# Hybrid encoder on one core: modulation's sums pinned in VectorE's order, three kinds of loads moved to later jobs

## The chip, the cores and the metric

One Trainium2 chip, one of its cores. The metric is the device time of one launch in microseconds (us). The kernel before was run three times.

## What is computed

Two layers (DEPTH = 2) of a hybrid encoder over one sequence of 256 tokens with 1024 features, all in f32. Cut to what matters here:

```python
for l in range(DEPTH):
    mod = (silu(c) @ w_ada[l] + b_ada[l]).reshape(bsz, 6, 1, D_MODEL)      # modulation
    shift1, scale1, gate1 = mod[:, 0], mod[:, 1], mod[:, 2]
    shift2, scale2, gate2 = mod[:, 3], mod[:, 4], mod[:, 5]
    h = x * (1.0 + scale1) + shift1
    aq, ak, av, bq, bk, bv, cq, ck, cv, dx, dg, gl = split(h @ w_in[l])
    oa = window_gqa(rope(aq), rope(ak), av)
    ob = neighbourhood_attention(bq, bk, bv, b_rpb[l])                      # its biases
    oc = diff_attention(rope(cq), rope(ck), cv)
    od = rg_lru_branch(dx, dg, d_wa[l], d_wx[l])                            # recurrence, its weights
    mix = sum(sigmoid(gl) * (stack(oa, ob, oc, od) @ w_branch[l])) @ w_out[l]
    x = layer_norm(ALPHA * x + gate1 * mix)
    x = layer_norm(ALPHA * x + gate2 * peer_ffn(x * (1.0 + scale2) + shift2))
```

## The kernel before, in words

**Jobs.** The program is one list of jobs, built in order and run by the loop at the end of `_body`. Most jobs are one product: a 512 KB block of weights (`src`) is loaded into one of three `raw` buffers, split by ScalarE into a high part `whi` (L230) and by VectorE into the rest `wlo` (L233), and multiplied by TensorE in three passes (`prod`, L238 to L240: 24 matmuls of 256 columns). Loads run three blocks ahead and splits two jobs ahead. A load into a `raw` buffer (L1218) waits for the `wlo` split that read that buffer last. Layer 0 starts with eight `start_chunk` jobs, which make the modulated input `h`; then come 38 jobs of `w_in` for the four mixers, 32 for the gates, 16 of `w_branch` and 8 of `w_out`; this stretch is called mixing here. After it come LayerNorm, 16 query jobs, 128 jobs that read `p_u`, and 128 that read `p_v` (V jobs). Layer 1 repeats mixing and what follows.

**Modulation.** `ada_load` loads a 512 KB column block of `w_ada` (L254), `ada_sum` multiplies it on VectorE by silu(c), adds along the row and leaves one column of `mods` (L259, shown as CUSTOM_DVE_ANT_0 in the trace, as ISA in the instruction order). The eight first pairs (shift1 and scale1 of layer 0) are summed in `start_chunk`. The 24 next (gate1, shift2, scale2 of layer 0) are loaded and summed during layer 0's mixing: `stage(i)` hangs on the job `w[8 * i // 3]`, `staged(i)` on the job five later, with two buffers in `mixA`. All others (56) are loaded and summed beside V jobs into the tile `adav`, `vstage` on one job and the sum four jobs later. Layer 1's mixing holds no modulation.

**Who sets the order.** The program's text gives each instruction a place, and a scheduler then orders each engine's queue by its own estimate of when operands are ready; each engine runs its queue strictly in that order. `V` is VectorE, and its instructions can be moved. `VB` (class `InOrder`) issues the same instruction through `tc.keep_in_program_order`, so that it keeps its place in the text. In the trace all instructions issued through `VB` or `SB` carry line L93. The loads all go through one queue, SyncE's (SP), also in order: one that waits for its buffer holds all behind it.

**Mixing's own loads.** `mix_begin` loads the recurrence's weights `wblk` (1 MB, L437) into the buffer that held `x`, the cosines (256 KB, L442) and, by `load_bias`, the neighbourhood biases (two of 1 MB, L588). Rotary jobs (`rope_post`) copy rows by four small DMAs each (L460) and then do two products and a sum on VectorE (L465 to L467).

Of the kernel before, what the change touches and what calls it, by code (L numbers as in the profile page):

```python
# [18 lines left out]
OP = mybir.AluOpType  # L19
# [97 lines left out]
def _body(tc, nc, A, pp, big, hp, st, wk, ps, dr, stop, dump):  # L117
    V, S, PE = nc.vector, nc.scalar, nc.tensor
    VB, SB = InOrder(tc, V), InOrder(tc, S)
# [25 lines left out]
    state = {"left": [], "leaving": []}  # L145
# [83 lines left out]
    def split_hi(hi, src, scale=1.0):  # L229
        return S.activation(hi, src, AF.Copy, scale=scale)  # L230

    def split_lo(lo, src, hi):
        return V.tensor_tensor(lo, src, hi.bitcast(F32), op=OP.subtract)  # L233

    def prod(out, whi, wlo, x, n):

        for c in range(n):
            PE.matmul(out, wlo(c), x(c)[:, 0], start=c == 0, stop=False)  # L238
            PE.matmul(out, whi(c), x(c)[:, 1], start=False, stop=False)  # L239
            PE.matmul(out, whi(c), x(c)[:, 0], start=False, stop=c == n - 1)  # L240
# [12 lines left out]
            with behind(state["load"]):  # L253
                nc.sync.dma_start(buf[:, k], A["w_ada"][l, i, :, k * D:(k + 1) * D])  # L254

    def ada_sum(l, i, buf, ks=(0, 1)):
        for k in ks:
            n = ADA[2 * i + k]
            V.tensor_tensor_reduce(out=buf[:, k], in0=buf[:, k], in1=state["cact"], scale=1.0,  # L259
                                   scalar=prm[:, P_BADA + 48 * l + n:P_BADA + 48 * l + n + 1],  # L260
                                   op0=OP.mult, op1=OP.add, accum_out=mods[l][:, n:n + 1])

    def mains(ks):

        state["banks"] = cycle(ks)

    def main_bank(shape, name):
        return bank(next(state["banks"]), shape, name=name)
# [25 lines left out]
    def new_h():  # L294
        return hp.tile([128, NC8, 2, T], F32R, name="h", tag="h")
# [86 lines left out]
    jobs = []  # L382
# [7 lines left out]
            before[n + 1 + i].hooks.append(lambda i=i, j=j: area_split(i, j))  # L390

    def start_chunk(m):
        ada_sum(0, m, state["ada"][:, m])
        if m == 0:
            state["h"] = new_h()
        hx = state["h"]
        x = state["x"][:, m]
        V.tensor_scalar(opsc[:, m:m + 1], mods[0][:, 8 + m:9 + m], 1.0, None, op0=OP.add)
        h = wk.tile([128, T], F32, name="hf", tag="t1k", bufs=6)
        S.activation(h, x, AF.Identity, scale=opsc[:, m:m + 1], bias=mods[0][:, m:m + 1])  # L400
        split_hi(hx[:, m, 0], h)
        split_lo(hx[:, m, 1], h, hx[:, m, 0])
# [20 lines left out]
    def layer(l):  # L423
# [3 lines left out]
        def mix_begin():  # L427
            m = big.tile([128, 64, T], F32, name="mixA", tag="gA")
            state["m"] = m
            state["bh"] = [big.tile([128, 12, 2, T], F32R, name="mixB0", tag="gB0"), None]  # L430
            state["gt"] = big.tile([128, 32, T], F32, name="mixG", tag="gB1")
            mains((0, 1, 5))
            state["ab"] = []
            state["scans"] = 0
            mf = m.rearrange("p a b -> p (a b)")
            state["wblk"] = big.tile([128, 16, 128], F32, name="wblk", tag="gB2")
            nc.sync.dma_start(state["wblk"], A["d_w"][l])  # L437
            state["dxp"] = mf[:, 34 * 256:34 * 256 + 4 * 260].rearrange("p (c t) -> p c t", c=4)
            V.memset(state["dxp"][:, :, 0:2], 0.0)
            V.memset(state["dxp"][:, :, 258:259], 0.0)  # L440

            nc.sync.dma_start(state["gt"][:, 6:8].rearrange("p a b -> p (a b)"), A["cst"][:, C_COS:C_COS + 2 * T])  # L442
            load_bias()

        def w_in_job(n, post):
            def mm(hi, lo):
                out = main_bank([128, T], name="main")
                state["out"] = out
                x = state["h"]
                prod(out, lambda c: hi[:, c], lambda c: lo[:, c], lambda c: x[:, c], NC8)  # L450
                return out
            return Job(src=A["w_in"][l, n], mm=mm, post=post)

        def rope_post(n, slot, scale):
            def post(out):
                dst = state["m"][:, slot]
                rot = wk.tile([128, T], F32, name="ropet", tag="t1k", bufs=6)
                S.activation(dst, out, AF.Copy, scale=scale)
                for a, b in ((0, 32), (32, 0), (64, 96), (96, 64)):
                    nc.sync.dma_start(rot[a:a + 32], dst[b:b + 32])  # L460

                def gen(lane):
                    yield 0.0
                    cos, sin = state["gt"][:, 6], state["gt"][:, 7]
                    V.tensor_tensor(dst, dst, cos, op=OP.mult)  # L465
                    V.tensor_tensor(rot, rot, sin, op=OP.mult)
                    V.tensor_tensor(dst, dst, rot, op=OP.add)  # L467
                state["leaving"].append(gen)
            return post

        def copy_post(slot, scale=1.0):
            def post(out):
                S.activation(state["m"][:, slot], out, AF.Copy, scale=scale)
            return post

        def v_post(dst):
            def post(out):
                raw = wk.tile([128, T], F32, name="vx", tag="t1k", bufs=6)
                S.activation(raw, out, AF.Copy)

                def gen(lane):
                    yield 0.0
                    p = bank(2, [128, 2, 128], name="vt")
                    for t in range(2):
                        PE.transpose(p[:, t], raw[:, t * 128:(t + 1) * 128], ident)
                    V.tensor_copy(dst(), p)
                state["leaving"].append(gen)
            return post

        def vdst(slot, n, k):  # L490
            def f():
                v = state["m"][:, slot:slot + n].rearrange("p a b -> p (a b)").rearrange("p (t e) -> p t e", t=2)
                return v[:, :, k * 128:(k + 1) * 128]
            return f
# [89 lines left out]
        def load_bias():  # L584
            b = state["m"][:, 39:55].rearrange("p a b -> p (a b)").rearrange("p (t h k) -> p t h k", h=8, t=2)
            state["bias"] = b
            for t in range(2):
                nc.sync.dma_start(b[:, t].rearrange("p h k -> p (h k)"), A["rpb"][l, t])  # L588
# [54 lines left out]
        def lru(lane):  # L643
# [28 lines left out]
            for d, (tr, ti, aa) in enumerate(parts):  # L672
                for c in range(4):
# [12 lines left out]
                    yield 0.4, 2.8  # L686

        jobs.append(Job(func=mix_begin))
        first = len(jobs)
        def add(name, *gens):  # L690
# [7 lines left out]
            jobs.append(w_in_job(DG + c, gelu_post(30 + c)))  # L698
        for c in range(4):
            jobs.append(w_in_job(AQ + c, rope_post(AQ + c, c, 0.125)))  # L700
        jobs.append(w_in_job(AK, rope_post(AK, 4, 1.0)))
        jobs.append(w_in_job(AV, v_post(vdst(21, 1, 0))))
        for c in range(4):
# [5 lines left out]
        add("lru", lru)  # L709
        for c in range(4):  # L710
            jobs.append(w_in_job(BQ + c, copy_post(5 + c, 0.125)))
        for c in range(4):
            jobs.append(w_in_job(BK + c, copy_post(9 + c)))
        for c in range(4):
# [75 lines left out]
        def staged(i):  # L790
            buf = state["m"][:, 55:63].rearrange("p (a b) c -> p a (b c)", a=2)
            ada_sum(l, 8 + i // 2, buf, (i % 2,))
        w = [j for j in jobs[first:] if j.src is not None][4:]
        for i in range(24 if l == 0 else 0):
            w[8 * i // 3].hooks.append(lambda i=i: stage(i))
            w[8 * i // 3 + 5].hooks.append(lambda i=i: staged(i))
# [349 lines left out]
        vjobs = []  # L1146
        todo = [(l, 20 + i) for i in range(4)] + ([(l + 1, i) for i in range(20)] if l + 1 < DEPTH else [])

        def vstage(i, k):
            if i == k == 0:  # L1150
                both = hp.tile([128, 2, 2, D], F32, name="adav", tag="h")
                for n in range(2):
                    state["ada", n] = both[:, n]
            ada_load(*todo[i], state["ada", i % 2], k)
# [7 lines left out]
        for i in range(len(todo)):  # L1162
            for k in range(2):
                n = (10 if len(todo) < 12 else 5) * i + 2 * k
                vjobs[n].hooks.append(lambda i=i, k=k: vstage(i, k))
                vjobs[n + 4].hooks.append(lambda i=i, k=k: ada_sum(*todo[i], state["ada", i % 2], (k,)))

        if l + 1 < DEPTH:
            state["vjobs"] = vjobs
# [22 lines left out]
    for m in range(NC8):  # L1192
        jobs.append(Job(func=lambda m=m: start_chunk(m)))
    jobs.append(Job(func=start_end))
    jobs.append(Job(func=late_setup))
    for l in range(DEPTH):
        layer(l)
# [4 lines left out]
    if stop is not None:  # L1202
        jobs = jobs[:stop(jobs)]
# [44 lines left out]
    k = 0  # L1248
    last = None
    for i, j in enumerate(jobs):  # L1250
# [29 lines left out]
        out = j.mm(hi, lo)  # L1280
# [93 lines left out]
```

## Time and profile before

| what | us |
|---|---|
| three runs: median (lowest to highest) | 2356.8 (2355.9 to 2358.27) |
| the profiled execution: its own time | 2358.0 |
| the profiled execution: span of the core's instructions | 2356.2 |
| TensorE busy (14440 matmuls) | 2275.3 |
| VectorE busy | 1813.7 |
| ScalarE busy | 1414.0 |
| granted TensorE clock, mean over the span | 0.986 of full |

The profiled execution lies 1.2 us above the median. Its span starts with the first instruction and ends with the last; 1.8 us of its time lie around it. A matmul's busy time runs until its modelled end, so that matmuls overlap; what the engine lost shows in the idle time ahead of an instruction and in the granted clock.

### The profile page before, as it was taken

The page shows a single profiled execution, that of the slowest core. Times are in us where ns is not written, and L with a number is a line of the kernel's source. Part 1 is how long each engine was busy: PE and PEld are TensorE (multiplying, and loading weights), DVE is VectorE, ACT ScalarE, POOL GpSimd, SP SyncE. Part 2 cuts the span into 40 slices and gives each one's busy share as a digit, 9 for nine tenths or more (in the row PEclk, how much of TensorE's full clock was granted, in tenths as well). Part 3 has the DMA queues.
Part 4 walks back from the last instruction along what each step waited for, and adds up shares of the span by engine and source line. Part 5 has one row for each costly group of instructions (what it writes and reads, how often), then busy time and mean ns, then how long its engine had stood idle before and what let it go on. Part 6 is the DMA issues. An engine that isn't in the chain of part 4 may idle for free.

```text
span 2356.2 us, 40963 instructions
## 1 busy us (share of the span) xinstructions
PE 2275.3 (97%) x14440; PEld 2008.4 (85%) x14440; DVE 1813.7 (77%) x3919; ACT 1414.0 (60%) x3067; POOL 220.6 (9%) x260
## 2 busy tenths in 40 slices
PE   5999999999999999999989999999999999999997
PEld 4889898988888878888889999898888888888886
DVE  7778688998889777777766676889888896665555
ACT  5566545577776754545556665456777776545544
POOL 0000000132222200000000000002222222000000
PEclk9999999999999999999999999999999999999998
DMA  9665555688888988888754544648888899766563
GB/s 354 220 204 197 180 170 175 196 227 203 209 205 203 230 261 275 262 292 293 254 181 156 153 162 156 199 150 210 220 205 205 205 213 236 234 212 194 192 213 108
DMA packets 165324, 495.46 MB, mean 210 GB/s; under 512 B 19584, under 2 KB 57216, under 8 KB 161920
## 3 DMA queue, kind: packets, MB, share of 16 engines
q1 hardware_dynamic: 127248, 453.51, 60.3%
q0 software_dynamic: 36864, 33.57, 9.5%
q10 hardware_dynamic: 1008, 5.77, 0.7%
q8 instruction: 115, 1.88, 0.3%
q14 instruction: 89, 0.73, 0.1%
HBM read 450.57 MB, written 5.24 MB: 193 GB/s over the span
## 4 chain that ended last, share of the span: by engine, by line
PE 81%; DMA 7%; DVE 7%; ACT 3%; issue 2%; SPq 0%; POOL 0%; ACTq 0%; DVEq 0%; POOLq 0%
PE main L246 18%; PE main L247 9%; PE vacc L1102 9%; PE vacc L1103 9%; PE vacc L1104 9%; PE main L238 7%; PE main L239 7%; PE main L240 7%; DVE wlo L233 2%; DMA mixA<-in_w_ada 1%; PE gw L1002 1%; PE gw L1003 1%; DVE topk L93 1%; DMA raw<-in_w_in 1%; ACT whi L230 1%
## 5 line engine op out<-in xcount | busy, mean ns | idle before, releaser
L233 DVE TENSOR_TENSOR wlo<-raw,whi 128x1024 fp32r<-128x1024 f32 x723 | 879.5, 1218 | 323.3 <-ACT whi L230 319.6
L230 ACT ACTIVATE whi<-raw 128x1024 fp32r<-128x1024 f32 x720 | 763.5, 1060 | 557.0 <-PE vacc L1104 262.0
L246 PE MATMUL main<-h,whi 128*128 128x512 f32 x2048 | 733.1, 401 | 1.1 <-ACT whi L230 1.1
L247 PE MATMUL main<-h,wlo 128*128 128x256 f32 x2048 | 574.3, 281 | 2.0 <-DVE wlo L233 2.0
L246 PEld LDWEIGHTS main<-h,whi 128*128 128x128 f32 x2048 | 385.2, 188 | 86.4 <-ACT whi L230 1.4
L238 PE MATMUL main<-h,wlo 128*128 128x256 f32 x1408 | 410.9, 293 | 6.4 <-DVE wlo L233 5.7
L1102 PE MATMUL vacc<-whi,wv 128*128 128x512 f32 x1024 | 399.0, 390 | 2.4 <-DVE wv L233 2.4
L240 PE MATMUL main<-h,whi 128*128 128x256 f32 x1408 | 400.5, 285 | 0.0
L239 PE MATMUL main<-h,whi 128*128 128x256 f32 x1408 | 400.3, 285 | 0.0
L1103 PE MATMUL vacc<-wlo,wv 128*128 128x512 f32 x1024 | 399.2, 390 | 1.0 <-DVE wlo L233 1.0
L1104 PE MATMUL vacc<-whi,wv 128*128 128x512 f32 x1024 | 398.6, 389 | 0.0
L247 PEld LDWEIGHTS main<-h,wlo 128*128 128x128 f32 x2048 | 387.1, 189 | 3.6 <-DVE wlo L233 3.3
L1059 POOL DMA_DIRECT2D u<-more x256 | 220.4, 861 | 1766.5 <-DMA raw<-in_p_u 1198.8
L238 PEld LDWEIGHTS main<-h,wlo 128*128 128x128 f32 x1408 | 271.6, 193 | 12.2 <-DVE wlo L233 7.9
L239 PEld LDWEIGHTS main<-h,whi 128*128 128x128 f32 x1408 | 272.1, 193 | 0.5
L240 PEld LDWEIGHTS main<-h,whi 128*128 128x128 f32 x1408 | 271.8, 193 | 0.1
L1102 PEld LDWEIGHTS vacc<-whi,wv 128*128 128x128 f32 x1024 | 192.1, 188 | 43.8 <-DVE wv L233 4.1
L1103 PEld LDWEIGHTS vacc<-wlo,wv 128*128 128x128 f32 x1024 | 192.3, 188 | 42.7 <-DVE wlo L233 3.3
L1104 PEld LDWEIGHTS vacc<-whi,wv 128*128 128x128 f32 x1024 | 192.2, 188 | 40.1
L1057 ACT ACTIVATE more<-main 128x256 f32<-128x256 f32 x256 | 96.4, 377 | 7.8 <-PE main L247 7.8
L984 DVE TENSOR_TENSOR ohe<-iota,ijg 128x1024 f16<-128x1024 f16 x128 | 87.5, 686 | 17.5 <-PE gw L1003 17.5
L259 DVE CUSTOM_DVE_ANT_0 adav<-adav,cact,prm 128x1024 f32<-128x1024 f32 x56 | 71.9, 1284 | 36.0 <-DMA adav<-in_w_ada 35.5
(236 smaller groups left out, 2753.5 us busy)
## 6 DMA issues: line engine op xcount, KB each, us to landing
raw<-in_p_u SPq DMA_DIRECT2D x256, 512.0 KB, 4.5
raw<-in_p_v SPq DMA_DIRECT2D x256, 512.0 KB, 4.2
raw<-in_w_in SPq DMA_DIRECT2D x134, 512.0 KB, 3.9
u<-more POOLq DMA_DIRECT2D x256, 128.0 KB, 5.2
adav<-in_w_ada SPq DMA_DIRECT2D x56, 512.0 KB, 5.5
raw<-in_w_br SPq DMA_DIRECT2D x32, 512.0 KB, 3.5
raw<-in_p_wq SPq DMA_DIRECT2D x26, 512.0 KB, 3.6
mixA<-in_w_ada SPq DMA_DIRECT2D x24, 512.0 KB, 4.7
```

Source lines behind the costliest of these rows:

```text
L230: return S.activation(hi, src, AF.Copy, scale=scale)
L233: return V.tensor_tensor(lo, src, hi.bitcast(F32), op=OP.subtract)
L238: PE.matmul(out, wlo(c), x(c)[:, 0], start=c == 0, stop=False)
L239: PE.matmul(out, whi(c), x(c)[:, 1], start=False, stop=False)
L240: PE.matmul(out, whi(c), x(c)[:, 0], start=False, stop=c == n - 1)
L246: PE.matmul(out, whi(c), x(c), start=c == 0, stop=c == n - 1, skip_group_check=True)
L247: PE.matmul(out[:, 0], wlo(c), x(c)[:, 0], start=False, stop=c == n - 1, skip_group_check=True)
L1057: S.activation(more, out[:, 1], AF.Copy)
L1059: nc.gpsimd.dma_start(u, more, accum_op=OP.add)
L1102: PE.matmul(o, wl[:, tt], hi, start=first, stop=False)
L1103: PE.matmul(o, wh[:, tt], lo, start=False, stop=False)
L1104: PE.matmul(o, wh[:, tt], hi, start=False, stop=last)
```

## The change

`ada_sum` takes the engine as an argument: `V` in `start_chunk`, `VB` everywhere else. The two products of the rotary jobs go through `VB` as well. The load of `wblk` moves from `mix_begin` to a job of its own after the first eight mixing jobs, and `load_bias` to one behind the four BQ jobs. The modulation of mixing starts on the eleventh mixing job instead of the fifth, and beside V jobs the sum hangs six jobs behind its load instead of four. No arithmetic changes, and no number of instructions.

```diff
-    def ada_sum(l, i, buf, ks=(0, 1)):
+    def ada_sum(l, i, buf, ks=(0, 1), engine=VB):
         for k in ks:
             n = ADA[2 * i + k]
-            V.tensor_tensor_reduce(out=buf[:, k], in0=buf[:, k], in1=state["cact"], scale=1.0,
+            engine.tensor_tensor_reduce(out=buf[:, k], in0=buf[:, k], in1=state["cact"], scale=1.0,
...
     def start_chunk(m):
-        ada_sum(0, m, state["ada"][:, m])
+        ada_sum(0, m, state["ada"][:, m], engine=V)
...
             state["wblk"] = big.tile([128, 16, 128], F32, name="wblk", tag="gB2")
-            nc.sync.dma_start(state["wblk"], A["d_w"][l])
...
-            load_bias()
...
-                    V.tensor_tensor(dst, dst, cos, op=OP.mult)
-                    V.tensor_tensor(rot, rot, sin, op=OP.mult)
+                    VB.tensor_tensor(dst, dst, cos, op=OP.mult)
+                    VB.tensor_tensor(rot, rot, sin, op=OP.mult)
...
             jobs.append(w_in_job(AQ + c, rope_post(AQ + c, c, 0.125)))
+        jobs.append(Job(func=lambda: nc.sync.dma_start(state["wblk"], A["d_w"][l])))
...
             jobs.append(w_in_job(BQ + c, copy_post(5 + c, 0.125)))
+        jobs.append(Job(func=load_bias))
...
-        w = [j for j in jobs[first:] if j.src is not None][4:]
+        w = [j for j in jobs[first:] if j.src is not None][10:]
         for i in range(24 if l == 0 else 0):
             w[8 * i // 3].hooks.append(lambda i=i: stage(i))
             w[8 * i // 3 + 5].hooks.append(lambda i=i: staged(i))
...
-                vjobs[n + 4].hooks.append(lambda i=i, k=k: ada_sum(*todo[i], state["ada", i % 2], (k,)))
+                vjobs[n + 6].hooks.append(lambda i=i, k=k: ada_sum(*todo[i], state["ada", i % 2], (k,)))
```

**What moves on the load queue.** SP's queue where layer 0's mixing begins, behind the last load of `late_setup`. Before:

```order
L588 DMA mixA<-in_rpb 128x2048
L442 DMA mixG<-in_cst 128x512
L588 DMA mixA<-in_rpb 128x2048
L437 DMA wblk<-in_d_w 128x2048
L1218 DMA raw<-in_w_in 128x1024 x3
L254 DMA mixA<-in_w_ada 128x1024
L1218 DMA raw<-in_w_in 128x1024
L460 DMA ropet<-mixA 32x256 x4
```

And now:

```order
L1218 DMA raw<-in_w_in 128x1024 x2
L441 DMA mixG<-in_cst 128x512
L586 DMA mixA<-in_rpb 128x2048
L699 DMA wblk<-in_d_w 128x2048
L586 DMA mixA<-in_rpb 128x2048
L1218 DMA raw<-in_w_in 128x1024 x2
L458 DMA ropet<-mixA 32x256 x4
```

Two loads of weights went ahead of the biases, the cosines and `wblk`, and no modulation load stands among the first weights; the first one comes behind the twelfth weight load of this queue instead of the sixth.

**What moves on VectorE.** VectorE's queue during the gates of layer 0, where the second head of the differential attention (`cw`) and the norm of the first (`msc`, `newton`) are under way. Before:

```order
L601 TENSOR_REDUCE cw<-s_2815 128x2
L602 TENSOR_SCALAR cw<-cw 128x2
L233 TENSOR_TENSOR wlo<-raw,whi 128x1024
L602 TENSOR_SCALAR cw<-cw 128x2
L259 ISA mixA,mods_78<-mixA,cact,prm 128x1024
L259 ISA mods_78 128x1
L607 RECIPROCAL cw<-cw 128x2x2
L630 TENSOR_SCALAR msc<-stc_2874 128x2
L608 TENSOR_SCALAR cw<-cw,lamv 128x2
L317 TENSOR_SCALAR newton<-msc 128x2
```

And now:

```order
L233 TENSOR_TENSOR wlo<-raw,whi 128x1024 x2
L93 ISA mixA,mods_78<-mixA,cact,prm 128x1024
L93 ISA mods_78 128x1
L599 TENSOR_REDUCE cw<-s_2809 128x2
L599 TENSOR_REDUCE cw<-s_2810 128x2
L600 TENSOR_SCALAR cw<-cw 128x2
L233 TENSOR_TENSOR wlo<-raw,whi 128x1024
L600 TENSOR_SCALAR cw<-cw 128x2
L605 RECIPROCAL cw<-cw 128x2x2
L606 TENSOR_SCALAR cw<-cw,lamv 128x2
```

The sum no longer stands between the head's maximum and its reciprocal; it stands behind the weights' splits, where the text has it. Counted over both queues, a sum stood behind the `wlo` split that is 0 to 3 later than the one that releases the weight load just ahead of its own load (in the 24 sums of mixing); now it is 5 later for each of the 24. Beside V jobs the count goes from mostly 3 to 6.

## Rows read from the trace of the kernel before

**Rows 1.** The page's first part: busy time of TensorE, share of the span.

```profile
PE 2275.3 (97%) x14440; PEld 2008.4 (85%) x14440; DVE 1813.7 (77%) x3919; ACT 1414.0 (60%) x3067; POOL 220.6 (9%) x260
```

**Rows 2.** Mixing by stretch, both layers: length; busy PE, PEld, DVE, ACT, POOL; PEclk.

```profile
42.03:376.20 334.17, 320.99 (x2550) 305.94 (x2550) 260.13 (x559) 192.24 (x368) 0.00 (x0) 0.98 0.62 207
1208.50:1524.05 315.55, 314.13 (x2562) 300.94 (x2560) 230.25 (x477) 188.24 (x366) 0.00 (x0) 1.00 0.54 175
```

**Rows 3.** Timeline, TensorE, layer 0's mixing: matmuls behind idle time [us, releaser].

```profile
51.12 0.39 PE L238 MATMUL main<-h,wlo 128*128 128x256 f32 x1 [1.60 <-DVE wlo L233]
56.14 0.39 PE L238 MATMUL main<-h,wlo 128*128 128x256 f32 x1 [1.89 <-DVE wlo L233]
71.81 0.38 PE L238 MATMUL main<-h,wlo 128*128 128x256 f32 x1 [1.03 <-DVE wlo L233]
...
137.51 0.41 PE L485 MATMUL vt<-ident,vx 128*128 128x128 f32 x2 [1.80 <-DVE mixA L486]
245.98 0.39 PE L238 MATMUL main<-h,wlo 128*128 128x256 f32 x1 [0.68 <-DVE wlo L233]
262.97 0.40 PE L324 MATMUL rbc<-ident,msc 128*128 128x128 f32 x2 [2.24 <-DVE msc L321]
277.49 0.80 PE L628 MATMUL stc<-ones,sqc 128*128 128x1 f32 x3 [1.90 <-ACT sqc L624]
```

**Rows 4.** Waits of TensorE in layer 1's mixing, 1199 to 1525 us: total, times, longest.

```profile
PE pt L513 <- DVE e L564: 0.5, 1, 0.5
PE vt L485 <- DVE mixA L486: 0.4, 1, 0.4
...
PE main L238 <- DVE wlo L233: 0.3, 1, 0.3
```

**Rows 5.** Timeline, SP's queue where layer 0's mixing begins.

```profile
36.56 0.33 SPq L588 DMA_DIRECT2D mixA<-in_rpb  x1
...
41.58 1.02 SPq L588 DMA_DIRECT2D mixA<-in_rpb  x1
45.65 0.33 SPq L437 DMA_DIRECT2D wblk<-in_d_w  x1
46.03 5.39 SPq L1218 DMA_DIRECT2D raw<-in_w_in  x3
```

**Rows 6.** Timeline, VectorE, then ScalarE: splits of weight blocks.

```profile
38.21 1.23 DVE L233 TENSOR_TENSOR wlo<-raw,whi 128x1024 fp32r<-128x1024 f32 x1 [0.45 <-ACT whi L230]
...
53.77 1.06 ACT L230 ACTIVATE whi<-raw 128x1024 fp32r<-128x1024 f32 x1 [3.83 <-DMA raw<-in_w_in]
69.44 1.06 ACT L230 ACTIVATE whi<-raw 128x1024 fp32r<-128x1024 f32 x1 [3.99 <-DMA raw<-in_w_in]
```

**Rows 7.** Waits of VectorE, 42 to 300 us: total, times, longest.

```profile
DVE mixA L259 <- DMA mixA<-in_w_ada: 22.7, 13, 4.9
```

**Rows 8.** Timeline, VectorE: sums of layer 0's mixing that waited for their load.

```profile
130.52 1.28 DVE L259 CUSTOM_DVE_ANT_0 mixA<-mixA,cact,prm 128x1024 f32<-128x1024 f32 x1 [2.63 <-DMA mixA<-in_w_ada]
237.97 1.29 DVE L259 CUSTOM_DVE_ANT_0 mixA<-mixA,cact,prm 128x1024 f32<-128x1024 f32 x1 [2.81 <-DMA mixA<-in_w_ada]
257.11 1.29 DVE L259 CUSTOM_DVE_ANT_0 mixA<-mixA,cact,prm 128x1024 f32<-128x1024 f32 x1 [4.34 <-DMA mixA<-in_w_ada]
270.98 1.29 DVE L259 CUSTOM_DVE_ANT_0 mixA<-mixA,cact,prm 128x1024 f32<-128x1024 f32 x1 [4.91 <-DMA mixA<-in_w_ada]
```

**Rows 9.** The line of modulation's loads (L254), 40 to 300 us: issue to landing.

```profile
DMA to landing us min/median/max: 4.0/4.7/6.6
```

**Rows 10.** The same view where layer 0's clock fell.

```profile
264.00:268.00 4.00, 4.00 (x23) 3.85 (x24) 2.03 (x4) 0.65 (x2) 0.00 (x0) 0.59 0.73 231
...
276.00:284.00 8.00, 6.51 (x30) 6.51 (x31) 6.70 (x20) 2.88 (x6) 0.00 (x0) 0.60 0.70 242
```

**Rows 11.** Waits beside V jobs, layer 0: VectorE's for modulation; TensorE's for a split.

```profile
DVE adav L259 <- DMA adav<-in_w_ada: 35.5, 35, 2.5
...
PE vacc L1103 <- DVE wlo L233: 0.5, 1, 0.5
```

## Prediction

> **What bounds the kernel.** I read the page first: TensorE is busy 97% of the span [rows 1], so only its own idle time, and time at a lower granted clock, can be won. Next I compared the same work in both layers. Mixing without its first three jobs takes 334.2 us in layer 0 and 315.6 us in layer 1, with about equal counts of matmuls [rows 2]: 18.6 us apart. Layer 1 has no modulation there, at a clock of 1.00 against 0.98, and its VectorE is busy 230.25 us against 260.13, the 29.9 us being the 24 sums of 1.28 us [rows 2, 8]. So 18.6 us is about what mixing can give back if layer 0 ran as smoothly as layer 1. Then I looked for those microseconds in TensorE's timeline [rows 3]: seven stops of 0.68 to 2.24 us, against three of 0.3 to 0.5 us within layer 1's mixing [rows 4]. All but one (the matmul behind `sqc`) name VectorE as the releaser. What VectorE itself waited for is the load of a modulation block: 22.7 us in 13 sums, up to 4.9 us at a time [rows 7, 8].
>
> **First part of the change: loads where mixing begins.** Before, SP issues biases, cosines, biases and `wblk` from 36.56 to 45.65 us, and the first three weight blocks behind them only from 46.03 us [rows 5]. They queue behind 3.25 MB (256 KB, two biases and `wblk` of 1 MB each), and ScalarE then sits 3.83 us until the first lands, at 53.77 us [rows 6]. TensorE stops 1.89 us for its split [rows 3]. Now two of the three blocks stand ahead of the four other loads; the split that freed the second of their buffers ended at 38.21 + 1.23 = 39.4 us [rows 6]. They have over 6 us more, over three times the stop, so I count 1.89 us as won. The stop of 1.03 us at 71.81 us goes back to a block that landed at 69.44 us, after 3.99 us of ScalarE waiting [rows 6]; modulation blocks that stood between the first weights are no longer there, and I count it as won too. Together 2.9 us; at worst 0, if the two blocks are as late as before. The stop of 1.60 us at 51.12 us stays: ScalarE is at the setup's small functions there, which don't move.
> What pays: `wblk` and the second bias block land later by two blocks' time. A block of 512 KB takes 4.7 us in the middle, overlapped with others [rows 9]; the recurrence starts behind the fourteenth product in the text, some nine products of 3.0 us (worked out below) after `wblk` goes out, and the biases are read later still, so over 20 us cover it. If the cover were gone, it would cost up to 4.7 us, once.
>
> **Second part: the sums keep their place.** Before, a sum came 0 to 3 `wlo` splits behind the point at which its load was let out; now 5 for each. A job is 24 matmuls, by rows 2 24 x 315.6 / 2562 = 3.0 us, so a sum now has about 15 us where a load lands after 4.0 to 6.6 us [rows 9]. I expect the 22.7 us of VectorE's waiting to go entirely. What of it lies on TensorE's path is in rows 3: the stop of 1.80 us follows the sum that waited 2.63 us (it ends at 131.8 us, and holds up the copies behind it); 0.68 us follows the one of 2.81 us; 2.24 us is the norm's `msc`, directly behind the sum of 4.34 us; 1.90 us follows the sum of 4.91 us through the next head's exponentials [rows 3, 8]. In each case the wait removed is longer than the stop it makes, so all of it goes: 1.80 + 0.68 + 2.24 + 1.90 = 6.6 us. The rest of the 22.7 us was beside TensorE's work and is worth nothing.
> After the last two of these stops the granted clock was at 1.2 GHz for a time: 0.59 of full over 264 to 268 us, and 0.60 over 276 to 284 us, of which TensorE was busy 6.51 us [rows 10]. Lost work: 4 x 0.41 + 6.51 x 0.40 = 4.2 us. Elsewhere in mixing after its beginning the stops were single and short; the fall came after the two longest that lie close together, so I count it as gone with them. Ends: 0 if the clock falls elsewhere, 4.2 if it doesn't.
> A rule against this: the Trainium skill, "DMA: Bandwidth & Descriptors", section "Anatomy of one DMA", gives for its gpsimd path some 2.0 us plus bytes over 436 GB/s, so by an estimate from that page 3.2 us for a block; loads so short would have made the old places late enough, and the second part would win nothing. The trace disagrees for these loads: 4.0 us is the least and 4.7 the middle [rows 9], and 13 sums did wait [rows 7].
>
> **Third part: rotary products pinned, V jobs.** In layer 1's mixing the pins change VectorE's order by a few rows, and the waits they could touch are 1.2 us in all [rows 4]: bounded by 1.2 us either way, taken as 0. Beside V jobs sums waited 35.5 us for loads, but TensorE only 0.5 us for a split [rows 11]: 0 to 0.5 us, taken as 0. In mixing the last four sums or so fall into the first `w_branch` jobs instead of the gates; VectorE has the same work there in another order, 260 of 334 us busy [rows 2], so 5 us of sums find room.
>
> **The sum.** 2.9 + 6.6 + 4.2 = 13.7 us. With its stops gone layer 0 still has the short ones of layer 1, so I take back 1.2 us [rows 4]: 12.5 us. Against the profiled execution's own 2358.0 us that is 2345.5; it lies 1.2 us above the median, so from the median of 2356.8 the forecast is **2344.3 us**. The 18.6 us of rows 2 hold this: what is left of them is the stop of 1.60 us, the low clock at mixing's very start, and small waits.
>
> **Rivals.**
> - *The clock falls elsewhere* (0.14). The stops go, but a new pair of waits in the heads brings the clock down for as long: 12.5 - 4.2 = 8.3 us, 2348.5. For it: the norm's chain is long. Against: 4.34 + 1.29 us leave VectorE ahead of `msc`, twice the stop.
> - *The waits behind the sums are the real ones* (0.10). VectorE's order around the heads changes, and `msc`, `sqc` and the copies come as late as before for ScalarE's sake; only the beginning is won: 2356.8 - 2.9 = 2353.9. For it: the last stop's releaser is ScalarE [rows 3].
> - *Loads were short enough* (0.03). If the loads took no longer than a job and the sums waited for something else that the profile puts down to them, the second part wins nothing: 2353.9. Rows 9 speak against it. The estimate from the Trainium skill's page "DMA: Bandwidth & Descriptors", named above, would make this of it.
> - *Nothing moves where it counts* (0.03). The two weight blocks share the engines with the same 3.25 MB, the sums' waits are covered anyway: 2356.8.
> - *SP is held* (0.04, slower). Each sum now stands directly behind the `wlo` split that also frees a weight buffer, and the next modulation load but one waits for that sum, with the weight loads queued behind it: 24 holds of 1.28 us, 30.7 us if none is covered, less the 12.5 us won: 2375.0. It decides once a hold passes more than 12.5 / 24 = 0.52 us to TensorE. A weight block is issued three jobs, 8.9 us, ahead of need and takes about 4.7 us, so 4.2 us of slack stand against 1.28; even at 6.6 us [rows 9] there are 2.3.
>
> **How the numbers follow.** The forecast has 0.66 and reaches from 2340 to 2349 us: below, 18.6 less the 1.60 us that stay give 17.0, so 2339.8; above, half of the stops or the clock stay. The range takes in the clock case and the two that end at 2353.9: 2339.5 to 2354. It leaves out the slower case, the case without effect, and a part of the forecast's edges, under 0.2 together. About 0.2% (4.7 us) is what a measurement of this kernel tells from no change. Faster by more: 0.66 + 0.14 = 0.80. Within: 0.10 + 0.03 + 0.03 = 0.16. Slower: 0.04.
>
> **What would show it.** Right: VectorE's waits for `in_w_ada` in mixing near 0; TensorE's rows at 56, 72, 137, 263 and 277 us without idle time; granted clock 1.00 from 100 to 370 us; layer 0's mixing within 6 us of layer 1's; layer 1 and the V jobs as long as before. Wrong: stops of TensorE behind `msc`, `sqc` or `vt` of over 1 us although no sum waited; a window of mixing at a clock near 0.6; waits of `whi` for weights while SP waits for a sum.

## Result, and the profile after

Side by side on one chip the kernel before took 2357.5 us (median of 4 runs, 2355.9 to 2359.87) and the changed one 2343.0 us (4 runs, 2341.5 to 2344.33): a ratio of 0.9937, 95% interval [0.9924, 0.995], so 14.5 us less. The profiled execution of the change took 2341.8 us, its span 2340.0, which is 16.2 us less than the span before.

The page of the changed kernel, its first part and the shares of the chain that ended last:

```profile
PE 2268.6 (97%) x14440; PEld 2004.8 (86%) x14440; DVE 1813.1 (77%) x3919; ACT 1414.4 (60%) x3067; POOL 220.6 (9%) x260
...
PE 88%; DVE 5%; DMA 4%; ACT 2%; issue 1%; SPq 0%; POOL 0%; ACTq 0%; DVEq 0%; POOLq 0%
```

The engines do the same work as before [rows 1]. What changed is the chain: 88% of it is TensorE, where it was 81%, with VectorE at 7% and DMA at 7%. The same line of the page before:

```profile
PE 81%; DMA 7%; DVE 7%; ACT 3%; issue 2%; SPq 0%; POOL 0%; ACTq 0%; DVEq 0%; POOLq 0%
```

The same work in stretches, after (columns as in rows 2; the layers' mixing without its first three jobs, then two stretches of layer 0):

```profile
41.78:360.77 318.99, 314.80 (x2550) 301.35 (x2550) 260.32 (x559) 192.11 (x369) 0.00 (x0) 0.99 0.66 219
1194.08:1509.67 315.59, 314.29 (x2562) 301.11 (x2562) 230.01 (x477) 188.36 (x366) 0.00 (x0) 1.00 0.55 175
...
264.00:268.00 4.00, 4.00 (x36) 4.00 (x35) 3.90 (x9) 1.42 (x2) 0.00 (x0) 1.00 0.48 137
276.00:284.00 8.00, 8.00 (x67) 7.89 (x66) 6.22 (x15) 5.12 (x11) 0.00 (x0) 1.00 0.76 237
```

Layer 0's mixing went from 334.2 to 319.0 us, layer 1's stayed at 315.6 [rows 2]. So 15.2 of the 16.2 us are in layer 0's mixing, and its distance to layer 1 fell from 18.6 to 3.4 us. The two stretches that ran at 0.59 and 0.60 of the full clock [rows 10] run at 1.00; TensorE does 36 and 67 matmuls there instead of 23 and 30.

TensorE's timeline after, 41 to 300 us: all matmuls behind more than 0.3 us of idle time:

```profile
41.78 0.58 PE L238 MATMUL main<-h,wlo 128*128 128x256 f32 x1 [0.56 <-ACT mixA L693]
50.87 0.38 PE L238 MATMUL main<-h,wlo 128*128 128x256 f32 x1 [1.63 <-DVE wlo L233]
60.65 0.38 PE L238 MATMUL main<-h,wlo 128*128 128x256 f32 x1 [0.89 <-DVE wlo L233]
76.57 1.13 PE L528 MATMUL s<-mixA 64*128 64x256 f32 x8 [0.33 <-DVE mixA L465]
84.20 0.41 PE L511 MATMUL pt<-ident,e 128*128 128x128 f32 x2 [0.72 <-ACT aw L546]
132.86 0.41 PE L483 MATMUL vt<-ident,vx 128*128 128x128 f32 x2 [0.37 <-DVE mixA L484]
```

Against rows 3: the stops at 56, 72, 246, 263 and 277 us are gone, and of the 1.80 us at 137 us 0.37 is left. The 1.63 us at 51 us stayed, and a new one of 0.89 us stands at 61 us. Rows 3 leave out the three shorter stops of the kernel before:

```profile
75.70 0.44 PE L485 MATMUL vt<-ident,vx 128*128 128x128 f32 x2 [0.75 <-ACT vx L479]
89.22 0.41 PE L513 MATMUL pt<-ident,e 128*128 128x128 f32 x2 [0.35 <-ACT mixG L663]
184.58 1.13 PE L660 MATMUL z<-mixG,wblk 128*128 128x256 f32 x4 [0.59 <-DVE mixA L486]
```

VectorE no longer waits for any `in_w_ada` block in 42 to 300 us, where it had waited 22.7 us in 13 sums [rows 7]. Its timeline shows sums with no idle time before them; the third line is the view of the loads' line (L254), 40 to 300 us:

```profile
253.33 1.28 DVE L93 CUSTOM_DVE_ANT_0 mixA<-mixA,cact,prm 128x1024 f32<-128x1024 f32 x1
264.85 1.28 DVE L93 CUSTOM_DVE_ANT_0 mixA<-mixA,cact,prm 128x1024 f32<-128x1024 f32 x1
...
DMA to landing us min/median/max: 3.7/4.7/6.4
```

The loads take as long as before [rows 9]; only the place of the sum changed. The chain of waits shows what that means. Here is the chain of the kernel before, 242 to 278 us (start, duration, what the end hung on), a piece that rows 3 and 8 show only from the side:

```profile
242.07 4.46 DMA mixA<-in_w_ada
...
247.85 2.28 DVE wlo L233 x2
...
250.53 6.55 DMA mixA<-in_w_ada
257.11 1.29 DVE mixA L259
...
260.46 1.14 DVE wlo L233
...
262.77 1.24 DVE wlo L233
...
264.41 6.55 DMA mixA<-in_w_ada
270.98 1.29 DVE mixA L259
...
273.65 1.02 ACT e L605 x4
...
277.49 1.02 PE stc L628 x4
```

And the chain of the change in the same place, 240 to 290 us, its shares by line first:

```profile
by line: PE main L238 27.8%; PE main L239 27.1%; PE main L240 27.0%; PE s L597 6.4%; PE oc L618 5.6%; PE pt L511 2.6%; PE stc L626 2.0%; PE rbc L324 1.6%
...
264.98 0.34 PE stc L626 x4
...
268.30 0.44 PE pt L511 x4
```

Before, the end hung for 17.6 of these 35.4 us on three modulation blocks in flight, passed on by sums (270.98 us), then by a head's exponentials (273.65 us) to TensorE's `stc` at 277.49 us. After, no other engine stands in the chain there.

### The profile page after: what moved, and what is told of

The parts are those of the page before. It is cut to its first block, busy times and chain, and to the rows that moved or that the text cites. A ratio compares the mean times of both kernels' runs of the same rounds, so it can differ in the third digit from the quotient of the medians.

```text
span 2340.0 us, 40963 instructions
## 1 busy us (share of the span) xinstructions
PE 2268.6 (97%) x14440; PEld 2004.8 (86%) x14440; DVE 1813.1 (77%) x3919; ACT 1414.4 (60%) x3067; POOL 220.6 (9%) x260
## 4 chain that ended last, share of the span: by engine, by line
PE 88%; DVE 5%; DMA 4%; ACT 2%; issue 1%; SPq 0%; POOL 0%; ACTq 0%; DVEq 0%; POOLq 0%
PE main L246 18%; PE vacc L1102 10%; PE vacc L1103 10%; PE vacc L1104 10%; PE main L247 9%; PE main L238 8%; PE main L239 8%; PE main L240 8%; PE gw L1002 1%; DVE wlo L233 1%; PE gw L1003 1%; DVE topk L93 1%; DMA raw<-in_p_u 1%; DMA raw<-in_w_in 1%; PE pt L511 1%
## 5 line engine op out<-in xcount | busy, mean ns | idle before, releaser
L1058 ACT ACTIVATE u<-main 128x256 f32<-128x256 f32 x256 | 99.1, 387 | 0.0
```

Of the source, the lines that this page charges most:

```text
L1058: S.activation(u, out[:, 0], AF.Copy)
```

## The experiments

Times are medians, ratios are against the kernel before on the same chip (its medians there: 2359.15 us beside the pins alone, all but the pins, and the sum one and three jobs behind; 2359.05 beside the moved loads alone, modulation from the fifth job, the small edits undone, and the later constants; 2357.92 beside the later start alone, pins and later start, and the two kernels run again). Views of a trace are of one execution of each kernel.

**Which part pays.** Three edits were tried alone and in pairs. The sums pinned, nothing else:

```diff
-    def ada_sum(l, i, buf, ks=(0, 1)):
+    def ada_sum(l, i, buf, ks=(0, 1), engine=VB):
...
-            V.tensor_tensor_reduce(out=buf[:, k], in0=buf[:, k], ...
+            engine.tensor_tensor_reduce(out=buf[:, k], in0=buf[:, k], ...
...
-        ada_sum(0, m, state["ada"][:, m])
+        ada_sum(0, m, state["ada"][:, m], engine=V)
```

> Only the sums' pins on the kernel before; loads, their order and all jobs as before. Theory (sums that wait for their load on VectorE are what was lost): the count of splits between a load and its sum is 5 or 6 in mixing, VectorE's waits for in_w_ada fall from 22.7 us to under 2 us, the stops at 137, 246, 263 and 277 us and the low clock behind them go, the two stops at 56 and 72 us stay: 2345 to 2348 us. Rival (the earlier weight blocks and the modulation's later start bring it): 2355 to 2358 us.

Measured: 2346.0 us, ratio 0.9951 [0.9937, 0.9964]. VectorE's waits for modulation are gone, the late stops are gone, and the clock stays at 1.00 after 100 us; the stops at the start stay (1.62 us at 55.53, 0.94 at 71.12). So the pins give by far the largest part, by themselves.

All of the change but the pins:

```diff
-    def ada_sum(l, i, buf, ks=(0, 1), engine=VB):
+    def ada_sum(l, i, buf, ks=(0, 1), engine=V):
```

> The change without the sums' pins (rotary products stay pinned). Theory: the scheduler sets the sums 1 to 3 splits behind their loads again, VectorE waits 15 to 25 us for in_w_ada in mixing, stops of 4 to 8 us and some low clock stay: 2350 to 2356 us. Rival (loads): 2343 to 2346 us.

Measured: 2350.4 us, ratio 0.9962 [0.9948, 0.9975]. The time fell inside what was expected, the reason did not: VectorE waited only 5.5 us, in 5 sums, and the clock did not fall. The other edits had changed where the scheduler put the sums: 1 to 3 splits behind their release instead of 0 to 3. That this is the reason is not shown: the kernel with only the later start, below, has the same count for each sum and 14.0 us of waits.

The loads of `wblk` and of the biases moved, nothing else:

```diff
-            nc.sync.dma_start(state["wblk"], A["d_w"][l])
...
-            load_bias()
...
+        jobs.append(Job(func=lambda: nc.sync.dma_start(state["wblk"], A["d_w"][l])))
         jobs.append(w_in_job(AK, rope_post(AK, 4, 1.0)))
...
+        jobs.append(Job(func=load_bias))
         for c in range(4):
             jobs.append(w_in_job(BK + c, copy_post(9 + c)))
```

> On the kernel before, only the loads of the recurrence's weights and of the biases go to their later jobs; modulation's start, sums and rotary products as before. Theory: two weight blocks go ahead of the 3.25 MB, the stop of 1.9 us at 56 us goes, the sums still wait 15 to 25 us on VectorE and the stops and low clock from 137 to 286 us stay: 2 to 3 us below before, ratio 0.9985 to 0.9995. Rival (the loads are most of the change): ratio 0.9935 to 0.996.

Measured: 2357.5 us, ratio 1.0001 [0.9988, 1.0014]. Nothing shows; the interval leaves room for less than 3 us. TensorE's timeline in this kernel:

```profile
61.06 0.39 PE L238 MATMUL main<-h,wlo 128*128 128x256 f32 x1 [1.24 <-DVE wlo L233]
64.62 0.39 PE L238 MATMUL main<-h,wlo 128*128 128x256 f32 x1 [0.42 <-DVE wlo L233]
71.75 0.39 PE L238 MATMUL main<-h,wlo 128*128 128x256 f32 x1 [1.11 <-DVE wlo L233]
...
263.01 0.40 PE L324 MATMUL rbc<-ident,msc 128*128 128x128 f32 x2 [1.58 <-DVE msc L321]
277.70 1.01 PE L626 MATMUL stc<-ones,sqc 128*128 128x1 f32 x4 [3.55 <-ACT sqc L622]
```

The stop at 56 us went, and 1.24 + 0.42 us came at 61 and 65 us. The first weights go out early, but the third and fourth blocks now queue behind the 3.25 MB, the fourth behind a modulation block as well, and the products that need them stop instead. The late stops stay, and with them the low clock.

The change with modulation from the fifth job again, and the converse, the kernel before with only the later start. First the former:

```diff
-        w = [j for j in jobs[first:] if j.src is not None][10:]
+        w = [j for j in jobs[first:] if j.src is not None][4:]
```

> The change with mixing's modulation from the fifth job again instead of the eleventh. Theory: the sums are 4 to 7 splits behind their loads whatever job they start on, so no waits come back in mixing; only modulation's blocks are among the first weights again, for a stop of up to 1 us near 70 us: 0 to 1.5 us slower than the change, ratio 0.9935 to 0.9945. Rival (the later start keeps VectorE or the queue free where it counts): 3 us or more slower, ratio 0.995 or more.

Measured: 2349.3 us, ratio 0.9954 [0.994, 0.9967], 4 us more than the change by the ratios; the change was run on other chips, and the intervals overlap. The kernel without the small edits (below, 0.9931 on this chip) is 5.4 us faster. No sum waits for its block, as expected, but the loss is over 1.5 us: the later start is worth more than that.

The latter:

```diff
-        w = [j for j in jobs[first:] if j.src is not None][4:]
+        w = [j for j in jobs[first:] if j.src is not None][10:]
```

> The kernel before with one edit: mixing's modulation starts on the eleventh mixing job; sums stay movable, loads stay where they were. In the instruction order a sum stands 1 to 3 splits behind its release instead of 0 to 3. Theory 'the later start also sets how the scheduler places the sums, and gives what all but the pins gave': VectorE's waits for in_w_ada about 5 us, clock stays near 1.00 from 100 us on, start's stops stay at about 1.7 to 2.5 us, 2350 to 2353 us, ratio about 0.997. Rival 'moving the weights' loads gave that': waits stay near 20 us, time 2354 to 2359.

Measured: 2354.2 us, ratio 0.9979 [0.997, 0.9988], between the two theories, and 14.0 us of VectorE's waits, in 9 sums, also between. The late stops of 2.56 us at 136 us and 1.30 at 253 us are still there, and 252 to 256 us runs at 0.70 of the clock.

Pins and later start together, without the moved loads, the pinned rotary products and the V jobs' edit; and the change itself again on the same chip:

```diff
-    def ada_sum(l, i, buf, ks=(0, 1)):
+    def ada_sum(l, i, buf, ks=(0, 1), engine=VB):
...
-        w = [j for j in jobs[first:] if j.src is not None][4:]
+        w = [j for j in jobs[first:] if j.src is not None][10:]
```

> The kernel before with the sums pinned and modulation starting on the eleventh mixing job; biases and wblk load where they did, rotary products and V jobs as before. Theory 'pins plus later start are the whole change, the weights' loads are worth nothing': same as the change, 2341 to 2345 us, ratio 0.993 to 0.995. Rival 'the moved loads of biases and wblk win the stop at 56 us (1.89 us) only together with the later start': 2344 to 2347 us, about 2 us above the change, a stop of over 1.5 us before 60 us still there.

> The changed kernel again, beside the others on one chip: ratio 0.993 to 0.995, some 2343 us.

Measured: 2343.0 us, ratio 0.9931 [0.9917, 0.9944], against 2343.7 us and 0.9933 [0.9919, 0.9946] for the change. Within the intervals, 3 us either way, two of its edits are the whole change. Between 42 and 80 us this kernel stops TensorE once, 2.74 us at 51 us, where the change stops 1.63 and 0.89 us. So the rival's stop before 60 us is there, but no cost of it shows against the change. The granted clock was 1.00 over 42 to 50 us here and 0.80 in the change's execution, so TensorE came sooner to the same split, which ends at 50.8 us in both; here it then ran at 0.50 from 51 to 54 us. Single stops of these first microseconds therefore don't price an edit.

The stretch 42 to 100 us separates the start from the rest (columns as in rows 2): the kernel before,

```profile
42.00:100.00 58.00, 52.11 (x404) 48.97 (x405) 45.53 (x111) 35.80 (x65) 0.00 (x0) 0.97 0.78 263
```

the pins alone,

```profile
42.00:100.00 58.00, 53.05 (x407) 49.97 (x407) 43.81 (x108) 33.79 (x61) 0.00 (x0) 0.95 0.78 257
```

the later start alone,

```profile
42.00:100.00 58.00, 53.98 (x430) 51.80 (x431) 45.14 (x110) 34.68 (x64) 0.00 (x0) 0.97 0.72 242
```

and the change:

```profile
42.00:100.00 58.00, 54.43 (x437) 52.23 (x438) 44.12 (x108) 34.76 (x65) 0.00 (x0) 0.97 0.73 258
```

404 matmuls are done before, 407 with pins, 430 with the later start alone, 437 with all. The matmuls differ in size, so the count gives no time. The time at which TensorE comes to one and the same matmul does: `vt`, which stands at 137.51 us in rows 3 and has 770 or 771 matmuls of the trace before it in each kernel. Pins alone, the change from the fifth job, the later start alone, pins and later start:

```profile
136.07 0.41 PE L485 MATMUL vt<-ident,vx 128*128 128x128 f32 x2 [0.37 <-DVE mixA L486]
```

```profile
136.53 0.41 PE L483 MATMUL vt<-ident,vx 128*128 128x128 f32 x2 [0.38 <-DVE mixA L484]
```

```profile
135.89 0.41 PE L485 MATMUL vt<-ident,vx 128*128 128x128 f32 x2 [2.56 <-DVE mixA L486]
```

```profile
133.22 0.41 PE L485 MATMUL vt<-ident,vx 128*128 128x128 f32 x2 [0.38 <-DVE mixA L486]
```

Less the stop in brackets, TensorE is there at 135.71 us before, 135.70 with the pins, 135.64 with the moved loads, 136.15 with the change from the fifth job; and at 133.33 us with the later start alone, 132.84 with pins and later start, 132.49 with the change. So by then the later start wins 2.4, 2.9 and 3.7 us, and the moved loads less than 0.5 us either way. The likely cause is modulation's two blocks that stood among the first weights (at 51 and 62 us in SP's queue of the pins-alone kernel), not the `wblk` and biases ahead of them; that the sums' own time on VectorE has no part in it is not shown.

By the ratios the parts add up, taken times 2357 us: pins 11.6 us (0.9951), later start 4.9 (0.9979; its interval is 2.8 to 7.1 us), together 16.5 against 16.3 measured (0.9931); each is known to 2 or 3 us either way. On top of the pins the moved loads add nothing that shows. With the later start and no pins the ratio is 0.9979, and 0.9962 with the moved loads and the small edits besides, but those two intervals overlap. VectorE's waits were 14.0 and 5.5 us there, and 22.7 before against 22.8 with the loads alone. The moved loads do not act through the places of the sums: counted over both queues as above, each of the 24 sums stands behind as many splits with these loads moved as without (0 to 3 in the kernel before and with the loads alone, 1 to 3 in the two kernels with the later start). Why 14.0 us became 5.5 at the same places stays open.

**How far behind its load a sum must stand.** The change with the sum one job behind, and three:

```diff
-            w[8 * i // 3 + 5].hooks.append(lambda i=i: staged(i))
+            w[8 * i // 3 + 1].hooks.append(lambda i=i: staged(i))
```

> The change, but in mixing the pinned sum hangs one job behind its load instead of five (1 to 3 splits by count). Theory: the pin alone does nothing, the distance does: VectorE waits 10 to 25 us for in_w_ada, TensorE's stops in mixing come to 3 to 8 us more than with the change, 2347 to 2355 us. Rival (what hurt was the sum's place between the heads' small operations, not its load): no more than 1 us from the change, 2342 to 2344 us.

Measured: 2351.5 us, ratio 0.9969 [0.9959, 0.998]. VectorE's waits, 42 to 300 us:

```profile
DVE mixA L93 <- DMA mixA<-in_w_ada: 13.0, 8, 3.6
```

```diff
-            w[8 * i // 3 + 5].hooks.append(lambda i=i: staged(i))
+            w[8 * i // 3 + 3].hooks.append(lambda i=i: staged(i))
```

> The change with the pinned sum three jobs behind its load (3 splits by count, about 9 us against loads of 4.0 to 6.6 us). Theory: the distance covers every load, waits for in_w_ada under 3 us, 2342 to 2345 us. Rival (five jobs are needed, since loads queue on SP behind others): waits of 8 us or more and 2346 us or more.

Measured: 2343.5 us, ratio 0.9938 [0.9925, 0.9952], no wait for modulation. So the pin alone is not the cure: a sum pinned too near its load gives back about half of the gain. Of the 7.3 us that are left the later start alone gives 4.9, so most of what the pins won is gone. What matters is the distance in time against the load's 3.7 to 6.4 us. Three jobs, 9 us, do; one, 3 us, does not. This also settles the rival of short loads: with one job of 3 us, 8 sums still waited, up to 3.6 us. By the estimate from the Trainium skill, "DMA: Bandwidth & Descriptors", section "Anatomy of one DMA", 3.2 us for a block on the gpsimd path, one job would have nearly been enough; the trace disagrees.

**The small edits.** Rotary products movable, V jobs' sums four behind, as before the change:

```diff
-                    VB.tensor_tensor(dst, dst, cos, op=OP.mult)
-                    VB.tensor_tensor(rot, rot, sin, op=OP.mult)
+                    V.tensor_tensor(dst, dst, cos, op=OP.mult)
+                    V.tensor_tensor(rot, rot, sin, op=OP.mult)
...
-                vjobs[n + 6].hooks.append(...
+                vjobs[n + 4].hooks.append(...
```

> The change with two of its parts undone: V jobs' sums four jobs behind their loads, and rotary products free in VectorE's order. Theory: neither lies on TensorE's path, the same as the change within 1.5 us, ratio 0.993 to 0.9945. Rival (the V jobs' 35.5 us of VectorE waiting were on the path after all): 2 us or more slower, though four pinned jobs (12 us and more) cover the loads too, so that this part of the rival needs the wait to be in the place, not in the load.

Measured: 2342.4 us, ratio 0.9931 [0.9918, 0.9944]: the same as the change. These edits are worth nothing that shows.

**What is left at the start.** The stop at 51 us was put down to ScalarE's setup functions, so the recurrence's constants were put into a job further on, behind the products and ahead of the recurrence:

```diff
+    def late_lam():
         lm = prm[:, P_LAM:P_LAM + 16]
...
+        if l == 0:
+            jobs.append(Job(func=late_lam))
         add("lru", lru)
```

> The change, and in addition the recurrence's constants (an exponential on ScalarE with its function tables, and the series on VectorE) are computed just ahead of the recurrence instead of in the setup. Theory: the stop left at 51 us (1.6 us) is ScalarE's tables and goes with them; what is left at 61 us may move: 1 to 2.5 us below the change, ratio 0.9925 to 0.9935. Rival (the block that comes next is late anyway, so the stop only moves by a job): within 0.5 us of the change.

> The change with the recurrence's constants computed later, again, beside the change on the same chip. If its gain is real: 2.5 to 4.5 us below the change, ratio about 0.992. If it was scatter of the earlier batch: within 1 us of the change.

Measured: 2339.5 us, ratio 0.9919 [0.9906, 0.9931], and in the second batch 2340.3 us, 0.9922 [0.9908, 0.9935]: 3.4 us below the change beside it. In the first batch the change itself was not run; the kernel without the small edits, on that chip, was 2.9 us slower. The intervals of the ratios overlap; both batches agree, though, in size and sign. ScalarE's timeline in the change, then in the second of these:

```profile
44.95 1.28 ACT L195 ACT_TABLE_LOAD   x1
46.25 0.22 ACT L195 ACTIVATE sp<-sp 128x16 f32<-128x16 f32 x1
46.48 1.28 ACT L693 ACT_TABLE_LOAD   x1
...
48.06 1.05 ACT L230 ACTIVATE whi<-raw 128x1024 fp32r<-128x1024 f32 x1
...
58.28 1.06 ACT L230 ACTIVATE whi<-raw 128x1024 fp32r<-128x1024 f32 x1 [3.86 <-DMA raw<-in_w_in]
```

```profile
45.03 1.06 ACT L231 ACTIVATE whi<-raw 128x1024 fp32r<-128x1024 f32 x1
...
47.84 1.28 ACT L196 ACT_TABLE_LOAD   x1
49.13 0.21 ACT L196 ACTIVATE sp<-sp 128x16 f32<-128x16 f32 x1
...
55.94 1.06 ACT L231 ACTIVATE whi<-raw 128x1024 fp32r<-128x1024 f32 x1 [3.31 <-DMA raw<-in_w_in]
```

In the change a function of 0.22 us brings two table loads of 1.28 us ahead of the split at 48.06 us. With the edit that split is at 45.03 us, and the function comes behind it at 49.13 us with one table load: the scheduler still runs it near the start, though its job stands far down the list. The split's buffer is then free 3 us sooner, and the block that ScalarE waits for lands sooner too (its split starts at 55.94 instead of 58.28 us). The stop at 51 us is gone, and those at 58 and 62 us are 0.34 and 0.54 us. This kernel is the fastest of the study.

## Why the prediction held, and which step did not

Forecast 2344.3 us, measured 2343.0, inside the range; 12.5 us were forecast and 14.5 measured. Point by point, from the two profiled executions:

- *Sums' waits, 6.6 us:* right. The stops of 1.80, 0.68, 2.24 and 1.90 us became 0.37, 0, 0 and 0, and 0.59 us at 184.58 us, which the sum left out, went too: 6.84 us. The path of the last one is shown in the chain above, and from the other side by ScalarE: `e` at 273.65 us waited 4.46 us for VectorE's `cw` before, 1.09 us at 274.15 us after.
- *Low clock, 4.2 us:* right, and a little small. Both stretches are at 1.00, and the pins alone did this. The term took 0.60 as the clock of TensorE's busy time, but that mean takes in idle time. Read microsecond by microsecond, the clock was at 0.50 from 264 to 267 and from 278 to 284 us, with parts of the microseconds beside them, and 5.0 us of work were lost.
- *Start, 2.9 us:* about the right size, by luck, for a reason that was half wrong. The stops of 42 to 100 us over 0.3 us (without the one at 42 us) sum to 1.60 + 1.89 + 1.03 + 0.75 + 0.35 = 5.62 us before and to 1.63 + 0.89 + 0.33 + 0.72 = 3.57 after, 2.05 us won; by its arrival at `vt`, TensorE is 3.2 us ahead. The step that failed is "they have over 6 us more, over three times the stop, so I count 1.89 us as won". It looked at the two blocks that go first and not at the next, which queue behind the same 3.25 MB: ScalarE still waits 3.86 us for a block, only at 58.28 us. That edit alone gave nothing that shows, nor did it beside the others. The other half, modulation's blocks no longer among the first weights, was counted at 1.03 us and is worth 2.4 to 3.7 us at `vt`, 4 to 5 by the ratios.
- *The 1.60 us at 51 us stays:* right (1.63), and its cause, ScalarE's setup, is what the last edit took away.
- *Third part, 0:* right. Layer 1's mixing took 315.6 us in both. Beside V jobs VectorE's 35.5 us of waits [rows 11] went to none, and the time did not notice.
- *1.2 us taken back:* not needed. The short stops that remain are in the 3.57 us and the 0.37 us already. With 6.84 + 5.0 + 2.05 = 13.9 us, 1.3 of mixing's 15.2 us are left. They are not in idle time: that fell from 13.2 to 4.2 us (length less busy time, rows 2 and their lines after), and the 8.9 us of the stops are nearly all of it. About 1 us lies in busy time at full clock, and what it is stays open.

Of the rivals, the clock did not fall elsewhere (1.00 from 100 to 360 us); the waits behind the sums were not the real ones, since the late stops went with the pins alone; and the slower one, SP held by sums, did not come: ScalarE's waits for weights in 42 to 300 us are 9.6 us in 6, the last of them over at 72.03 us, just after the first modulation block was issued (71.4 us) and so before any sum.

What stays open: that last 1 us, and whether the later start is worth the 2.4 to 3.7 us seen at `vt` or the 4 to 5 us of the ratios. What it wins behind `vt`, if anything, can't be read from the kernel with it alone, whose profiled execution was the fastest of its runs (2349.7 us, median 2354.2).

## What to carry to other kernels

An instruction that waits for a load holds everything behind it on its engine (here, by way of VectorE, the exponentials at 273.65 us for 4.46 us), so its place must be a load's time behind the load's release. Where a scheduler sets the order by its own estimate, pin the instruction, and take the distance from measured landings (here 9 us against at most 6.6). Moving bulk loads behind the first weights was worth nothing here, because the blocks after the first two then queued behind them: follow the queue until the stop is gone, and test each such edit by itself.

## What the runs showed that was not expected

- Some stops of TensorE took the granted clock down, and their length does not tell which. In the kernel before it was at 0.50 of 2.4 GHz, the lower level of 1.2 GHz, behind the stops of 2.24 and 1.90 us [rows 3, 10]; in the moved-loads kernel at 0.50 from 278 to 282 us behind one of 3.55 us; in the later-start kernel at 0.50 in 254 to 256 us behind one of only 1.30 us, at 252.71 us. But it stayed at 1.00 in the later-start kernel behind 2.56 us at 135.89 us, in the moved-loads kernel behind 2.19 us at 137.83 us, and before behind 1.80 us at 137.51 us. What decides is open. Two stretches of the later-start kernel, columns as in rows 2:

```profile
136.00:138.00 2.00, 2.00 (x13) 1.76 (x14) 1.64 (x4) 0.01 (x1) 0.00 (x0) 1.00 0.07 16
254.00:256.00 2.00, 2.00 (x12) 2.00 (x11) 1.97 (x7) 0.90 (x1) 0.00 (x0) 0.50 0.95 381
```

- The place of a free sum, counted in splits, does not tell how long it waits. VectorE's waits for modulation were 22.7 and 22.8 us in two kernels whose sums stand at the same counts, but 14.0 and 5.5 us in two others that agree in this as well. As long as the sums are free, one timeline prices such an edit badly.
